# Query and key parts kept in one DRAM region each: a stack is fetched by one transfer of two runs of rows instead of by two transfers

## The chip, the cores and the metric

The kernel runs on one core of a Trainium2 chip. The metric is the device time of one execution in microseconds; the time of a kernel is the median of its runs. The engines of the core have names in the profile: PE does matrix products (PEld is its loading of weights, which runs beside the products), DVE and ACT do vector work, POOL and SP mostly issue transfers. A transfer (DMA) is issued by one engine into a queue of that engine and is carried by up to 16 DMA engines that all queues share.

## The reference, cut to what matters

Two layers of an encoder over 512 tokens of width 1024, in float32. Each layer is a SwiGLU feed-forward block of width 2816 at half weight, a mixer, and a second such block, each between two RMS norms. The mixer is what the change touches:

```
proj = u @ w_in            # q, k, v of three attention branches, and three gates
A: neighbourhood attention, 8 heads of 64, with a relative position bias
B: sliding window attention, 8 query heads and 2 key/value heads of 64, window 128
C: differential attention, 4 heads, two softmax maps each, rotary positions
m   = sum_i gate_i * (branch_i @ W_branch_i)
h   = h + post(m @ W_out)
```

## The kernel before, in words

**Precision.** Each float32 operand of a product is split into a high part `hi`, rounded to a narrower type that PE multiplies fast, and a low part `lo`, the rest. A product is then hi·hi + hi·lo + lo·hi: three matmuls (L326 to L328), mostly of 128 rows against 512 columns. The feed-forward blocks and most projections go through a scheme with fewer block products (L680), the gates of the mixer through the plain one (`dense1`, L345).

**Stacks.** A head has 64 rows (its width) and 512 columns (the tokens). Since 64 is half of PE's 128 rows, scores are made with *stacks*: tiles `st` of 128 rows with the 64 rows of `hi` of one head above the 64 rows of `lo` of the same head. A key head has a second stack with the two the other way round. One query stack against the two key stacks then gives all the products that are wanted, in two matmuls (L1675).

**From projection to mixer.** `project` makes the query, key and value parts of a layer, each 128 rows (two heads) by 512 tokens. For the first query and key part of branch A (`QA`, `KA`) it makes the stacks at once and leaves them on the chip, in slots called `early`. Every other part of branches A and B (queries QA+1 to QA+3 and QB to QB+3, keys KA+1 to KA+3 and KB) goes to DRAM by `stacked` (L1411): `store("part", hi)` and `store("part", lo)` put two regions of 128 rows, 256 KB each, by transfers that POOL issues (L1405). `mixer` fetches them: `restacked` (L1774) makes each stack with two transfers of 64 rows (128 KB), both issued by SP (L1783 the upper half, L1784 the lower half). A layer fetches 14 query stacks and 16 key stacks, so it issues 60 such transfers. Values are read whole (`values` and `load`, L1757), the relative position tables of branch A by `ask` (L1729, tile `braw`): each as 128 rows of 2 KB which the source gives as 8 runs of 16 rows. The query and key parts of branch C are stored whole, and `rope` (L1763) reads them as one transfer `x <- raw` and four `sh <- raw`, and turns them on DVE (L1769).

**What sets the order.** The mixer's units stand in a string `ORDER` (L93): `qa1` fetches what the second pair of heads of branch A needs, `aa1` computes them, `ga0` is a block of gates, `kb` and `qb0` fetch the key and the first query part of branch B, and so on. A scheduler orders the instructions of each engine by a model of their durations, so that dense gate products lie between the steps of an attention head. Once built, the order on an engine is fixed: an engine that has to wait at an instruction doesn't take up a later one. SP issues its transfers in order too, and there are eight semaphores in turn for the transfers that SP and ACT issue: a transfer waits until the one eight places earlier has landed. Weights (`wr`, 512 KB) are issued by ACT during the mixer (L211). There are 14 buffers `st`.

`softmax_pv` holds the steps of one attention head: scores (L1675), bias and row minimum on DVE (L1678), exponentials on ACT, transposes on PE (L1706), a split into `hi` and `lo` (L353 for `lo`), and the products with the values (L1709 with `hi`, L1710 with `lo`).

Of the kernel before, what the change touches and what calls it, by code (L numbers as in the profile page):

```python
# [10 lines left out]
F32 = mybir.dt.float32  # L11
# [5 lines left out]
P = 128  # L17
# [3 lines left out]
T = 512  # L21
# [18 lines left out]
QA, KA, VA, QB, KB, VB, QC, KC, VC, GL = 0, 4, 8, 12, 16, 17, 18, 22, 26, 30  # L40
# [79 lines left out]
def encoder_kernel(ctx: ExitStack, tc: tile.TileContext, order, xT, wts, cols, rows, rpb, consts, tables, out):  # L120
    nc = tc.nc
# [5 lines left out]
    dr = ctx.enter_context(tc.tile_pool(name="dr", bufs=1, space=bass.MemoryType.DRAM))  # L127
# [19 lines left out]
    def nm(s):  # L147
        serial[0] += 1
        return f"{s}{serial[0]}"

    def big(tag, dt=F32, shape=(P, T), name="v"):
        if tag in BUFS:
            return sb.tile(list(shape), dt, tag=tag, name=nm(name), bufs=BUFS[tag])
        kind, pool = phase[0]
        return pool.tile(list(shape), dt, tag=tag, name=nm(name), bufs=ABUFS[kind][tag])
# [7 lines left out]
    V, A, G, PE = nc.vector, nc.scalar, nc.gpsimd, nc.tensor  # L163

    def f(t):
        return t.bitcast(F32)
# [94 lines left out]
    for l in range(L):  # L261
        for which in (1, 2):
            name = f"ffn{which}_w_down"
# [1104 lines left out]
    def project(l, op, accs):  # L1368
# [34 lines left out]
        def store(kind, x):  # L1403
            d = dr.tile([P, T], F32, tag=kind, name=nm(kind), bufs=60)
            G.dma_start(d, f(x))  # L1405
            return d

        def parts(x):
            hi, lo = big("t", F32R, name="hi"), big("t", F32R, name="lo")
            A.activation(hi, x, AF.Copy)  # L1410
            V.tensor_tensor(out=lo, in0=x, in1=f(hi), op=ALU.subtract)  # L1411
            return hi, lo

        def stacked(c, x):
            hi, lo = parts(x)
            if c in (QA, KA):
                made[c] = []
                for s in range(2):
                    own, res = slice(64 * s, 64 * s + 64), []
                    for one, two in ((hi, lo), (lo, hi))[: 1 if c == QA else 2]:  # L1420
                        st = slots.pop(0)
                        nc.sync.dma_start(f(st)[0:64], f(one)[own])
                        nc.sync.dma_start(f(st)[64:128], f(two)[own])
                        res.append(st)
                    made[c].append((res + [None])[:2])
                return
            made[c] = store("part", hi), store("part", lo)

        def turned(c, x, heads):
            tp = bank("at")  # L1430
# [19 lines left out]
        def turned_by(c, x):  # L1450
            sh = big("t", name="sh")
            for q in range(4):
                o = q ^ 1
                nc.sync.dma_start(sh[32 * q : 32 * q + 32], x[32 * o : 32 * o + 32])
            slowly.extend(
                (
                    lambda: V.tensor_tensor(out=x, in0=x, in1=turning[0], op=ALU.mult),
                    lambda: V.tensor_tensor(out=sh, in0=sh, in1=turning[1], op=ALU.mult),
                    lambda: V.tensor_tensor(out=x, in0=x, in1=sh, op=ALU.add),
                    lambda: stacked(c, x),  # L1460
                )
            )

        def ready(c, x):
            if c >= GL:
                gated(c, x)
            elif c < VA:
                stacked(c, x)
            elif QB <= c < VB:
                turned_by(c, x)  # L1470
            elif c < KB or c >= VB and (c < QC or c >= VC):
                values.append(lambda: turned(c, x, 1 if c >= VC else 2))
            else:
                made[c] = store("raw", x)
# [11 lines left out]
        made = {}  # L1486
# [38 lines left out]
        for n, c0 in (("cosR", 0), ("sinR", 512)):  # L1525
            t = big("rr", name=n)
# [25 lines left out]
        def tables_of_a():  # L1552
            t = sb.tile([P, 4, T], F32, tag="n", name=nm("pre"), bufs=BUFS["n"])
            nc.sync.dma_start(t[:, 0, :], tables[:, 1024 : 1024 + 512])
            nc.sync.dma_start(t[:, 1, :256], tables[:, 1024 + 512 : 1024 + 768])
            for hd in range(2):
                nc.sync.dma_start(t[:, 2 + hd, :], raw_of(l, hd))
            made["tables"] = t
            made["edges"] = sb.tile([P, 4, T], F32, tag="n", name=nm("edges"), bufs=BUFS["n"])
# [75 lines left out]
        work(len(slowly))  # L1635
        return made

    def raw_of(l, hd):
        return bass.AP(rpb.tensor, (l * 8 + hd) * 16 * RPBW, [[RPBW, 8], [1, 16], [1, 8 * RPBW]])

# [76 lines left out]
    def mixer(l, op, made):  # L1717
# [6 lines left out]
        def ask(hd):  # L1724
            if hd < 2:
                raws[hd] = pre[:, 2 + hd, :]
                return
            raw = raws[hd] = big("g", name="braw")
            nc.sync.dma_start(raw, raw_of(l, hd))  # L1729
# [44 lines left out]
        def restacked(c, both):  # L1774
            if c in (QA, KA):
                return made[c]
            hi, lo = made[c]
            res = []
            for s in range(2):
                own, pair_ = slice(64 * s, 64 * s + 64), []  # L1780
                for one, two in ((hi, lo), (lo, hi))[: 2 if both else 1]:
                    st = big("st", F32R, name="st")
                    nc.sync.dma_start(f(st)[0:64], one[own])  # L1783
                    nc.sync.dma_start(f(st)[64:128], two[own])  # L1784
                    pair_.append(st)
                res.append((pair_ + [None])[:2])
            return res
# [20 lines left out]
        def qkv_a(p):  # L1808
            got = restacked(QA + p, False), restacked(KA + p, True), values(VA + p)
            for s in range(2):  # L1810
                ask(2 * p + s)
            return got
# [124 lines left out]
        def qkv_b(c):  # L1937
            return restacked(c, c == KB)
# [69 lines left out]
        at = len(order) // HB  # L2008
# [62 lines left out]
    for l in range(L):  # L2071
        with open_phase("f"):
            X, accs = ffn(l, 1, X, accs)
        with open_phase("p"):
            made = project(l, X, accs)
# [10 lines left out]
def build(order):  # L2086
    import concourse.bacc as bacc

    nc = bacc.Bacc("TRN2", target_bir_lowering=False, num_devices=1)
    shapes = {  # L2090
        "xT": (D, T),
        "wts": (NTILES, P, WB * P),
        "cols": (P, NCOLS),
        "rows": (L * ROWW,),
        "rpb": (L * 8 * 16 * RPBW,),
        "consts": (P, CONSTW),
        "tables": (P, TABLEW),
    }
    args = [nc.dram_tensor(f"in_{n}_dram", s, F32, kind="ExternalInput").ap() for n, s in shapes.items()]
    args.append(nc.dram_tensor("out_0_dram", (D, T), F32, kind="ExternalOutput").ap())  # L2100
    with tile.TileContext(nc) as tc:
        encoder_kernel(tc, order, *args)
    return nc
# [35 lines left out]
```

## Time and profile before

| what | value |
|---|---|
| time, median of 3 runs | 2371.69 us (2371.62 to 2374.82) |
| the profiled execution's own time | 2370.88 us |
| its span in the trace | 2369.1 us |
| instructions in the trace | 40269 |
| granted TensorE clock, mean | 0.996 |
| DMA over the span | 395.16 MB, mean 167 GB/s |
| stack transfers issued by SP, both layers | 120 of 128 KB |

The page gives busy times of the engines over the span, then the span cut into 40 slices, then the DMA queues, then the chain of work that ended last, then groups of instructions by line. The queue `q1` is SP's, `q10` ACT's, `q0` POOL's. In the table of stretches of time each engine has its busy time with the number of instructions, and behind them stand the granted clock of PE, the mean busy share of the 16 DMA engines, and GB/s. In the list of instructions in order of time a row has the start, the duration, the engine, the line, the operation, output and inputs, the shapes, and in square brackets how long the engine was idle before it and what ended that.

The two layers run the same program. The first score from a fetched stack of branch A starts at 531.18 us in the first layer and at 1703.59 us in the second, 1172.41 us later.

### The profile page before, as it was taken

What the parts mean: (1) busy time and instruction counts of PE and PEld (TensorE: products, weight loads), DVE (VectorE), ACT (ScalarE), POOL (GpSimd) and SP (SyncE); (2) the same over time, 40 slices, a digit from 0 to 9 for tenths busy, and PEclk for the clock granted to TensorE, in tenths of its full rate; (3) what the DMA queues carried; (4) which work ended last, traced back from release to release, by engine and by line L of the source; (5) the groups of instructions that cost most, each with busy time, mean ns of one, the idle gap of its engine ahead of it and who ended that gap; (6) DMA issues with size and microseconds to landing.
All of it is one profiled execution on the core that took longest, in us unless ns stands there. A gap on an engine that the chain in (4) does not pass through costs nothing. (4 is left out here: it accounts for less than half of the span.)

```text
span 2369.1 us, 40269 instructions
## 1 busy us (share of the span) xinstructions
PE 2342.6 (99%) x15134; PEld 2109.5 (89%) x15134; DVE 1892.4 (80%) x3082; ACT 1446.8 (61%) x2715; POOL 223.8 (9%) x354
## 2 busy tenths in 40 slices
PE   9999999999999999999999999999999999999998
PEld 8999889997888889998899998889978788899987
DVE  7887988966888668888878878889579876788796
ACT  6555566667777465655655554666687764556563
POOL 0111001110121001110001110011101200011100
PEclk9999999999999999999999999999999999999999
DMA  5566446667565524664525565276774664256642
GB/s 170 162 169 190 154 145 187 207 219 207 168 174 189 167 97 147 166 162 165 175 87 168 162 178 196 102 216 199 222 206 139 195 206 140 97 147 172 190 148 84
DMA packets 138147, 395.16 MB, mean 167 GB/s; under 512 B 19296, under 2 KB 26080, under 8 KB 137440
## 3 DMA queue, kind: packets, MB, share of 16 engines
q1 hardware_dynamic: 102960, 260.37, 35.0%
q0 software_dynamic: 20160, 78.66, 12.4%
q10 hardware_dynamic: 14832, 53.56, 7.4%
q8 instruction: 119, 1.95, 0.3%
q14 instruction: 76, 0.62, 0.1%
HBM read 326.98 MB, written 80.74 MB: 172 GB/s over the span
## 5 line engine op out<-in xcount | busy, mean ns | idle before, releaser
L680 PE MATMUL mm<-X,h 128*128 128x256 f32 x1504 | 268.0, 278 | 1.2 <-DVE v L738 1.2
L680 PEld LDWEIGHTS mm<-X,h 128*128 128x128 f32 x1504 | 228.5, 188 | 2.5 <-DVE v L738 2.0
L225 DVE TENSOR_TENSOR w<-wr,w 128x512 fp32r<-128x512 f32 x264 | 178.9, 685 | 56.2 <-ACT w L224 55.2
L224 ACT ACTIVATE w<-wr 128x512 fp32r<-128x512 f32 x264 | 162.5, 627 | 96.4 <-PE mm L328 40.8
L326 PE MATMUL mm<-X,w 128*128 128x512 f32 (+1 forms) x570 | 218.3, 383 | 1.8 <-ACT X L553 1.8
L328 PE MATMUL mm<-X,w 128*128 128x512 f32 (+1 forms) x570 | 216.4, 380 | 0.8 <-DVE w L225 0.8
L327 PE MATMUL mm<-X,w 128*128 128x512 f32 (+1 forms) x570 | 216.2, 379 | 0.8 <-DVE X L554 0.7
L680 PE MATMUL mm<-ht,h 128*128 128x256 f32 x752 | 210.1, 279 | 0.0
L680 PE MATMUL mm<-ht,l 128*128 128x256 f32 x752 | 210.1, 279 | 0.0
L680 PE MATMUL mm<-lt,h 128*128 128x256 f32 x752 | 209.4, 278 | 0.0
L680 PE MATMUL mx<-ht,h 128*128 128x256 f32 x752 | 208.3, 277 | 0.6 <-ACT v L724 0.6
L680 PE MATMUL mm<-X,l 128*128 128x256 f32 x752 | 208.2, 277 | 0.0
L680 PE MATMUL mx<-ht,l 128*128 128x256 f32 x752 | 208.1, 277 | 0.0
L680 PE MATMUL mx<-lt,h 128*128 128x256 f32 x752 | 207.9, 277 | 0.0
L630 DVE TENSOR_TENSOR l<-wr,h 128x1024 fp32r<-128x1024 f32 x94 | 114.9, 1222 | 65.7 <-PE mm L680 65.7
L662 ACT ACTIVATE h<-wr 128x1024 fp32r<-128x1024 f32 x94 | 99.9, 1062 | 78.7 <-PE mx L680 55.5
L680 PE MATMUL at<-X,w 128*128 128x256 f32 x1128 | 144.2, 277 | 0.0
L680 PEld LDWEIGHTS mx<-ht,h 128*128 128x128 f32 x752 | 141.2, 188 | 1.4 <-ACT v L724 1.4
L680 PEld LDWEIGHTS mm<-ht,l 128*128 128x128 f32 x752 | 141.7, 188 | 0.1
L680 PEld LDWEIGHTS mm<-ht,h 128*128 128x128 f32 x752 | 141.7, 188 | 0.0
L680 PEld LDWEIGHTS mm<-lt,h 128*128 128x128 f32 x752 | 141.7, 188 | 0.0
L680 PEld LDWEIGHTS mx<-ht,l 128*128 128x128 f32 x752 | 141.2, 188 | 0.2 <-DVE l L640 0.2
(458 smaller groups left out, 6802.4 us busy)
## 6 DMA issues: line engine op xcount, KB each, us to landing
wr<-in_wts_dram SPq DMA_DIRECT2D x273, 512.0 KB, 4.6
wr<-in_wts_dram ACTq DMA_DIRECT2D x102, 512.0 KB, 4.1
sum<-in_wts_dram POOLq DMA_DIRECT2D x64, 512.0 KB, 5.3
st<-part SPq DMA_DIRECT2D x120, 128.0 KB, 5.1
ap<-in_wts_dram SPq DMA_DIRECT2D x20, 512.0 KB, 5.6
a<-kept SPq DMA_DIRECT2D x32, 256.0 KB, 6.3
ap<-sum SPq DMA_DIRECT2D x16, 512.0 KB, 4.3
x<-part SPq DMA_DIRECT2D x32, 256.0 KB, 3.8
```

The lines of the kernel that those rows point to most:

```text
L224: A.activation(hi, raw, AF.Copy)
L225: V.tensor_tensor(out=lo, in0=raw, in1=f(hi), op=ALU.subtract)
L326: PE.matmul(acc, w[0], x[0], start=start, stop=False)
L327: PE.matmul(acc, w[0], x[1], start=False, stop=False)
L328: PE.matmul(acc, w[1], x[0], start=False, stop=stop)
L630: V.tensor_tensor(out=w["l1"], in0=self.raws[g][0], in1=f(w["h1"]), op=ALU.subtract)
L662: A.activation(self.W[g]["h24"], self.raws[g][1], AF.Copy)
L680: PE.matmul(acc, ws[i], xs[j], start=start and k == m == 0, stop=stop and k == n - 1 and m == 2, skip_group_check=True,)
```

## The change

The two regions `part` of a query or key part become one region `both`, with `hi` in rows 0 to 127 and `lo` in rows 128 to 255; a key part has a third piece, `hi` again, in rows 256 to 383. POOL puts each piece by a transfer of its own. A stack of head s is then read from the region by one transfer: rows 64s to 64s + 63 of one piece and the same rows of the next piece, which lies 128 rows behind. For the swapped stack of a key the reading starts one piece later (lo, then the second copy of hi). `halves` writes that source as an access pattern of three levels: 2 runs, 64 rows of each, 512 columns of each. The transfer's target is the whole tile `st` of 128 rows.

```diff
@@ stacked
-            made[c] = store("part", hi), store("part", lo)
+            n = 2 + (KA <= c < VA or c == KB)
+            d = dr.tile([n * P, T], F32, tag=f"both{n}", name=nm("both"), bufs=60)
+            for at, t in enumerate((hi, lo, hi)[:n]):
+                G.dma_start(d[P * at : P * at + P], f(t))
+            made[c] = d
@@ project, mixer
+    def halves(d, row):
+        pitch = d.ap[0][0]
+        return bass.AP(d.tensor, d.offset + row * pitch, [[P * pitch, 2], [pitch, 64], [1, T]])
@@ restacked
-            hi, lo = made[c]
             res = []
             for s in range(2):
-                own, pair_ = slice(64 * s, 64 * s + 64), []
-                for one, two in ((hi, lo), (lo, hi))[: 2 if both else 1]:
+                pair_ = []
+                for n in range(2 if both else 1):
                     st = big("st", F32R, name="st")
-                    nc.sync.dma_start(f(st)[0:64], one[own])
-                    nc.sync.dma_start(f(st)[64:128], two[own])
+                    nc.sync.dma_start(f(st), halves(made[c], P * n + 64 * s))
                     pair_.append(st)
                 res.append((pair_ + [None])[:2])
             return res
```

A layer's 60 stack transfers of 128 KB become 30 of 256 KB, with the same bytes read, and POOL issues 4 stores more (the second copies of KA+1 to KA+3 and KB). Lines behind L1427 carry higher numbers in the changed kernel: L1675 becomes L1683, L1706 becomes L1714, L1709 and L1710 become L1717 and L1718, L1729 becomes L1737, and the stack transfer is L1790.

The scheduler places instructions anew. On SP, at the start of the first layer's mixer, these transfers follow each other before the change (`braw` are the position tables of branch A, `st` the stacks of its third pair of heads):

```order
L1729 DMA braw_5944<-in_rpb_dram 128x1x512
L1783 DMA st_6125<-part_4444 64x512
L1784 DMA st_6125<-part_4446 64x512
L1783 DMA st_6128<-part_4444 64x512
L1784 DMA st_6128<-part_4446 64x512
L1783 DMA st_6131<-part_4457 64x512
L1784 DMA st_6131<-part_4459 64x512
L1783 DMA st_6134<-part_4459 64x512
L1784 DMA st_6134<-part_4457 64x512
```

The same place on SP in the changed kernel, with the next `braw` as its last row:

```order
L1737 DMA braw_5931<-in_rpb_dram 128x1x512
L1790 DMA st_6112<-both_4443 128x1x512
L1790 DMA st_6114<-both_4443 128x1x512
L1790 DMA st_6116<-both_4455 128x1x512
L1790 DMA st_6118<-both_4455 128x1x512
L1790 DMA st_6120<-both_4455 128x1x512
L1790 DMA st_6122<-both_4455 128x1x512
L1737 DMA braw_6128<-in_rpb_dram 128x1x512
```

Each pair of rows has become one, and the six stacks stand directly between two position tables. On PE the order moves as well. Before, the products with the values of an early head (`hi` or `lo` against `early`) are followed by dense gate products (`mm`):

```order
L1709 MATMUL o_6186<-hi_6190,early_3957 128x2x128
L1710 MATMUL o_6186<-lo_6191,early_3957 128x2x128
L1709 MATMUL o_6186<-hi_6199,early_3957 128x256
L1710 MATMUL o_6186<-lo_6200,early_3957 128x256
L328 MATMUL mm_6302<-X_3648,w_6106 128x512
L326 MATMUL mm_6302<-X_3648,w_6106 128x512
L327 MATMUL mm_6302<-X_3649,w_6106 128x512
L328 MATMUL mm_6302<-X_3648,w_6106 128x512
L1709 MATMUL o_6186<-hi_6208,early_3957 128x256
```

In the changed kernel, at the same place:

```order
L1717 MATMUL o_6167<-hi_6171,early_3957 128x2x128
L1718 MATMUL o_6167<-lo_6172,early_3957 128x2x128
L1717 MATMUL o_6167<-hi_6180,early_3957 128x256
L326 MATMUL mm_6283<-X_3648,w_6093 128x512
L327 MATMUL mm_6283<-X_3649,w_6093 128x512
L1683 MATMUL mx_6149<-st_5917,st_5913 128x256
L1683 MATMUL mx_6149<-st_5919,st_5913 128x256
L328 MATMUL mm_6283<-X_3648,w_6093 128x512
L1683 MATMUL mx_6153<-st_5917,st_5913 128x256
L1683 MATMUL mx_6153<-st_5919,st_5913 128x256
```

The scores of the next heads (`mx`, from fetched stacks) have moved ahead of dense products. The same holds up to the first scores of branch B: from the first score out of a fetched stack to the first score of `qb0`, PE has 133 dense matmuls of 512 columns, 91 matmuls of 256 and 44 of 128 before the change, and 84, 92 and 46 after it. Both layers are moved in the same way.

## Prediction, before the changed kernel was run

> **What bounds the kernel now.** I read the page first, then the waits of PE and the list of PE's instructions around the longest of them, then SP's transfers and the stretches of time about the start of the mixer.
>
> ```profile
> span 2369.1 us, 40269 instructions
> PE 2342.6 (99%) x15134; PEld 2109.5 (89%) x15134; DVE 1892.4 (80%) x3082; ACT 1446.8 (61%) x2715; POOL 223.8 (9%) x354
> q1 hardware_dynamic: 102960, 260.37, 35.0%
> ```
>
> PE is busy for 2342.6 of 2369.1 us: only 26.5 us of idling can be won, and every wait that is added to PE is paid in full, since its order is fixed and it has no slack elsewhere. SP's queue q1 uses the 16 DMA engines to 35.0% on the mean, so on the mean there is room. PE's waits that have to do with the mixer's loads:
>
> ```profile
> PE o L1710 <- DVE lo L353: 6.9, 2, 3.7
> ```
>
> That is two waits, one in each layer, 6.9 us together. The list of PE's instructions about them, the first layer's and then the second's, and what DVE and SP did then:
>
> ```profile
> 540.63 0.40 PE L328 MATMUL mm<-X,w 128*128 128x512 f32 x1
> 540.86 0.39 PE L326 MATMUL mm<-X,w 128*128 128x512 f32 x1
> ...
> 557.87 0.58 PE L1710 MATMUL o<-lo,x 128*128 128x256 f32 x1 [3.67 <-DVE lo L353]
> ...
> 559.11 0.63 PE L327 MATMUL mm<-X,w 128*128 128x512 f32 x1
> ...
> 563.36 0.40 PE L328 MATMUL mm<-X,w 128*128 128x512 f32 x1
> 1729.85 0.39 PE L1710 MATMUL o<-lo,x 128*128 128x256 f32 x1 [3.21 <-DVE lo L353]
> 548.06 0.43 SPq L1760 DMA_DIRECT2D x<-raw  x1
> 556.73 0.69 DVE L1769 TENSOR_TENSOR x<-x,cosR 128x512 f32<-128x512 f32 x1 [5.60 <-DMA x<-raw]
> 550.00:560.00 10.00, 6.33 (x30) 5.09 (x31) 3.00 (x11) 5.76 (x19) 0.00 (x0) 0.83 1.00 247
> ```
>
> `x<-raw`, issued at 548.06, came so late that DVE stood at its rotation for 5.60 us, until 556.73, with the split `lo` that PE needed queued behind it. PE stood for 3.67 us and then ran at a lower granted clock (0.83 in that stretch). A dense product starts 0.23 us after the one before (540.63 to 540.86) when PE runs freely; from 559.11 to 563.36 ten of them took 4.25 us, 1.95 more than 2.3. So the stall costs 3.67 + 1.95 = 5.6 us in the first layer and 3.21 + about 1.95 = 5.2 in the second: 10.8 us, and it comes from late loads.
>
> **The change part by part.** *Fewer issues.* SP issues 30 transfers less in each layer. What an issue takes on SP, the two-run one by the nearest row, a load in runs, and POOL's stores:
>
> ```profile
> L1783 SPq DMA_DIRECT2D st<-part x60: 444/504/1117, 495.2 to 1769.5; - x60
> L1729 SPq DMA_DIRECT2D braw<-in_rpb_dram x12: 622/643/665, 526.5 to 1733.4; - x12
> L1405 POOL DMA_DIRECT2D part<-hi x30: 542/542/599, 375.1 to 1686.8; - x30
> ```
>
> Instead of 60 × 0.504 = 30 us SP spends some 30 × 0.643 = 19 us in a layer. That shortens no row of PE by itself: SP's 11 us lie beside PE's work, and are worth at most what the stall is, 10.8 us for both layers. The 4 stores more in a layer are 4 × 0.54 = 2.2 us on POOL, busy for 9%; they are made during the projection, under PE's products. Nothing for them.
>
> *Who carries a two-run load.* The bytes loaded are the same; what decides is over how many DMA engines a transfer is spread. No two-run load is in the trace. The nearest are `braw` (128 rows of 2 KB in 8 runs of 16 rows) and the old stack halves (64 plain rows). Two `braw` are issued at 526.52, and stacks behind them from 528 on. Stretches of 2.5 us, a look at the emptiest microsecond, and the landing times of stacks issued from 524 to 528 and from 528 to 532:
>
> ```profile
> 526.52 1.39 SPq L1729 DMA_DIRECT2D braw<-in_rpb_dram  x2
> 526.00:528.50 2.50, 2.50 (x14) 2.06 (x13) 0.60 (x2) 2.50 (x10) 0.00 (x0) 1.00 0.90 275
> 528.50:531.00 2.50, 2.50 (x14) 2.12 (x14) 0.58 (x2) 2.50 (x8) 0.54 (x1) 1.00 0.90 71
> 530.00:531.00 1.00, 1.00 (x6) 0.80 (x5) 0.58 (x2) 1.00 (x5) 0.00 (x0) 1.00 0.28 51
> 531.00:533.50 2.50, 2.50 (x20) 2.32 (x20) 2.31 (x5) 2.27 (x7) 0.54 (x1) 1.00 0.95 316
> ...
> st<-part SPq DMA_DIRECT2D x3, 128.0 KB, 2.6
> st<-part SPq DMA_DIRECT2D x4, 128.0 KB, 8.1
> ```
>
> With `braw` in the queue the rate falls from 275 to 71 GB/s and comes back to 316. At 530 to 531 only 0.28 × 16 = 4.5 engines are busy, though loads stand in the queue, and stacks behind it take 8.1 us instead of 2.6. So a load given in 8 runs isn't spread over all engines; my reading is that each run goes to one engine as a piece, 8 runs to at most 8 engines. By the same reading two runs go to two engines, and these carry 131 kB each for every stack, one behind the other. I assume the same two each time: since the rate fell with two `braw` in the queue, loads in runs don't seem to take turns over all engines (if they did, many stacks in the queue would keep all sixteen busy). That bounds the cost from both sides: 16 engines, as for plain rows (no cost), and 2 engines (each 8 times as long busy). I take 2: `braw` is of the changed load's kind, a source of three levels, and the old halves are not.
>
> [...]
>
> *The price of a kB on one engine.* Three rows: a saturated stretch later in the layer, the page's q1, and the mixer's start.
>
> ```profile
> 1940.00:1950.00 10.00, 10.00 (x51) 7.78 (x49) 4.38 (x8) 5.34 (x10) 0.00 (x0) 1.00 1.04 390
> DMA packets 6938, 14.06 MB, mean 220 GB/s; under 512 B 1104, under 2 KB 1104, under 8 KB 6933
> q1 hardware_dynamic: 5750, 9.88, 59.3%
> st<-part SPq DMA_DIRECT2D x44, 128.0 KB, 4.5
> braw<-in_rpb_dram SPq DMA_DIRECT2D x6, 256.0 KB
> ```
>
> 390 GB/s over 16 engines are 24.4 GB/s, 41 ns per kB. The page's q1 gives 0.35 × 16 × 2369.1 us / 260,370 kB = 51 ns; q1 in the stretch 516 to 580 us gives 0.593 × 16 × 64 / 9,880 = 61 ns, with loads in each other's way. With 14 engines nearly idle there is less in the way: I take 45, and 41 and 61 as ends.
>
> *What the two engines have to carry.* The last four rows above are of the stretch 516 to 580 us, which holds what the mixer needs up to the first scores of `qb0`: 44 halves, which are 22 stacks. On each of the two engines: 22 × 131.1 = 2884 kB of stacks; of all else (14.06 − 5.77 = 8.29 MB) a sixteenth, 518 kB; and since the six `braw` lie on 8 engines, another 98 kB. Together 3500 kB. At 45 ns that is 157.5 us (143.5 at 41; 213.5 at 61).
>
> ```profile
> 516.27 0.44 SPq L1783 DMA_DIRECT2D st<-part  x1
> 531.18 0.28 PE L1675 MATMUL mx<-st,st 128*128 128x256 f32 x1
> 531.30 0.28 PE L1709 MATMUL o<-hi,early 128*128 128x256 f32 x1
> ...
> 580.11 0.48 PE L1675 MATMUL mx<-st,st 128*128 128x256 f32 x2
> L1675 PE MATMUL mx<-st,st x74: 276/332/442, 577.9 to 646.8; 128*128 128x256 f32 x42, 128*128 128x384 f32 x32
> ```
>
> The stacks start at 516.27, so the last one that `qb0` needs lands at about 673.8. When would PE want it? The first score from a fetched stack is at 531.18. From there to `qb0`, the changed order has 84 matmuls of 512 columns (0.23 us each), 92 of 256 (0.12, by 531.18 to 531.30) and 46 of 128 (half of that, an estimate): 19.3 + 11.0 + 2.8 = 33.1 us, so 564.3. The same sum for the order before (133, 91 and 44) gives 44.2, with the stall's 5.6 581.0, and the trace has `qb0`'s scores at 580.11: the method holds. PE is late by 673.8 − 564.3 = 109.5 us in a layer. Dense products can't fill that, as PE doesn't take up a later row, and those that the new order has put behind the scores come after the wait.
>
> *Behind `qb0`* eight stacks are left at most, each 131.1 kB × 45 ns = 5.9 us, while the scores of branch B's eight heads are spread over 577.9 to 646.8, 8.6 us a head. With the sixteenth of all else on the two engines it about balances; I add nothing and keep up to 12 us a layer for the upper end.
>
> *The sum.* 2 × 109.5 = 219 us of waiting, less the 10.8 us of the old stall, which the new wait contains: 2370.9 + 208 = 2579, in the profiled execution's own time of 2370.88 us. The median of the three runs is 0.8 us above that: **2580 us**. With 41 ns the wait is 95.5 us a layer: 2552. With 51 it is 130.5: 2622; with 61, 2693.
>
> **The rivals.**
> *All 16 engines carry the two-run load (faster).* The target is a tile of 128 plain rows, like that of `x`, and if the target decides, a stack lands as the halves did. For it: a stack is one transfer of 256 KB, and fewer queue behind each other. Against it: `braw` has the same target, and it held up the queue. Then late `x<-raw` goes, which the new order puts later on DVE too, and with it the 10.8 us: 2361, chance 0.05. [...]
>
> *No change.* All engines carry it, but the stall goes over to another load of the crowded start, a position table or the first key of `qb0`, wanted some 16 us earlier: 2371, chance 0.04.
>
> *Eight engines, as for `braw` (slower, by little).* If the pieces are smaller than a run, 22 × 32.8 + 616 = 1337 kB lie on the busiest engine, 60 us at 45 ns. The last stack is there at 576.5, 12 us behind 564.3; less 5.4 us, twice: about 2384, chance 0.07. It decides once an engine's share passes 48 us / 45 ns = 1070 kB.
>
> **How the numbers follow.** The forecast has 0.84. Its range: 41 ns gives 2552, and some of the rest can be moved behind `qb0`, which takes off 20; at the other end 51 ns gives 2622, and branch B adds 2 × 12 and stacks that hinder each other more, up to the 61 ns end at 2693, which I don't take in full: 2530 to 2680. A change of 0.2% (4.7 us) is about what a measurement of this kernel can tell from none. Faster by more: 0.05; within: 0.04; slower: 0.84 + 0.07 = 0.91.
>
> **What would show it.** In the profile after, PE waits at L1683 for `st`, some 100 us a layer, its busy share falls to about 91%, and the slices at the start of both mixers show GB/s of 50 to 100. A stack takes several times 5 us from issue to landing, and issues of SP wait for the transfer eight places earlier. The wait at L1718 for `lo` is gone or small. It is wrong if stacks land within 3 to 6 us at 200 GB/s or more: then all engines carry them; or if the waits lie at DVE's rotation or bias with `st` in time. If the wait is there but of another size, the price per kB or the ledger is the term at fault.

## The result, and the profile after

The changed kernel takes 2579.29 us (median of 5 runs, 2578.99 to 2584.57), the kernel before beside it 2371.62: a ratio of 1.0888, 95% interval 1.0868 to 1.0908. It is slower by some 208 us, about 104 in each layer. The profiled execution took 2579.29 us, with a span of 2577.5.

The page of the changed kernel, its first lines and the row of SP's queue:

```profile
span 2577.5 us, 40225 instructions
PE 2381.7 (92%) x15134; PEld 2138.8 (83%) x15134; DVE 1899.2 (74%) x3082; ACT 1448.5 (56%) x2715; POOL 226.0 (9%) x362
PEclk9999999977899999999999999999678999999999
q1 hardware_dynamic: 101160, 260.36, 31.5%
```

PE's idle time went from 26.5 to 195.8 us, which is 169.3 of the 208.4 us that the span grew. The other 39.1 stand in PE's busy time (2342.6 to 2381.7 with the same 15134 matmuls): the row PEclk shows it at 6 to 8 tenths of its clock in two places, the starts of the two mixers. A matmul that starts alone also counts as busy for longer than one in a row (0.40 us, where the next one starts after 0.23 us in the kernel before), so how much of the 39.1 us is the clock isn't separated. Bytes on SP's queue are the same as before. The waits of PE, and DVE's longest for a load:

```profile
PE mx L1683 <- DMA st<-both: 89.2, 15, 20.9
PE mx L1683 <- DVE nmx L1686: 45.8, 6, 12.8
PE o L1717 <- ACT hi L352: 18.0, 2, 9.0
PE o L1717 <- DVE o L1721: 15.4, 2, 8.5
PE o L1718 <- DVE lo L353: 6.0, 4, 3.1
```

```profile
DVE bedge L1752 <- DMA braw<-in_rpb_dram: 70.3, 6, 21.1
```

The first row is PE waiting for stacks. The rest I read as the same lateness on a longer way: DVE waits 70.3 us for position tables that are queued behind stacks, and PE waits for what DVE and ACT make after that. Who carries the stacks is read from a stretch in which nothing else runs, and from the issues on SP:

```profile
574.00:576.00 2.00, 0.00 (x0) 0.00 (x0) 0.00 (x0) 0.00 (x0) 0.00 (x0) 0.98 0.13 50
647.00:661.00 14.00, 0.00 (x0) 0.00 (x0) 0.00 (x0) 0.00 (x0) 0.00 (x0) 0.50 0.21 73
```

```profile
L1790 SPq DMA_DIRECT2D st<-both x60: 490/5100/8902, 494.7 to 1963.8; - x60
```

From 574 to 576 us no engine works, stacks and position tables are queued, and the 16 DMA engines are busy to 0.13 on the mean: 0.13 × 16 = 2 engines, at 50 GB/s, 25 GB/s each. From 647 to 661 PE does nothing at all for 14 us. An issue of a stack takes 5.1 us on SP in the median (0.504 before): as I read it, SP is held up until the two engines have taken work off the queue.

### The profile page after: what moved, and what is told of

Read it like the earlier page. It is cut to its first block, busy times and chain, and to the rows that moved or that the text cites. A ratio compares the mean times of both kernels' runs of the same rounds, so it can differ in the third digit from the quotient of the medians.

```text
span 2577.5 us, 40225 instructions
## 1 busy us (share of the span) xinstructions
PE 2381.7 (92%) x15134; PEld 2138.8 (83%) x15134; DVE 1899.2 (74%) x3082; ACT 1448.5 (56%) x2715; POOL 226.0 (9%) x362
## 3 DMA queue, kind: packets, MB, share of 16 engines
q1 hardware_dynamic: 101160, 260.36, 31.5%
## 5 line engine op out<-in xcount | busy, mean ns | idle before, releaser
L680 PE MATMUL mm<-X,h 128*128 128x256 f32 x1504 | 268.1, 278 | 2.5 <-DVE v L738 2.5
L680 PEld LDWEIGHTS mm<-X,h 128*128 128x128 f32 x1504 | 228.4, 188 | 3.8 <-DVE v L738 3.1
L326 PE MATMUL mm<-X,w 128*128 128x512 f32 (+1 forms) x570 | 222.2, 390 | 2.4 <-ACT X L553 1.8
L327 PE MATMUL mm<-X,w 128*128 128x512 f32 (+1 forms) x570 | 221.3, 388 | 0.8 <-DVE X L554 0.7
L328 PE MATMUL mm<-X,w 128*128 128x512 f32 (+1 forms) x570 | 218.3, 383 | 0.0
L680 PE MATMUL mm<-ht,h 128*128 128x256 f32 x752 | 210.6, 280 | 2.3 <-ACT at L719 2.2
L680 PE MATMUL mm<-ht,l 128*128 128x256 f32 x752 | 210.1, 279 | 0.0
L680 PE MATMUL mm<-lt,h 128*128 128x256 f32 x752 | 209.4, 278 | 0.0
L680 PE MATMUL mx<-ht,h 128*128 128x256 f32 x752 | 208.3, 277 | 0.3 <-ACT v L724 0.2
L680 PE MATMUL mm<-X,l 128*128 128x256 f32 x752 | 208.2, 277 | 0.0
L680 PE MATMUL mx<-ht,l 128*128 128x256 f32 x752 | 207.9, 276 | 0.0
L680 PE MATMUL mx<-lt,h 128*128 128x256 f32 x752 | 207.9, 276 | 0.0
L1683 PE MATMUL mx<-st,st 128*128 128x256 f32 (+1 forms) x224 | 62.0, 373 | 135.1 <-DMA st<-both 89.2
L1683 PEld LDWEIGHTS mx<-st,st 128*128 128x128 f32 x224 | 46.6, 236 | 145.9 <-DMA st<-both 60.1
L680 PEld LDWEIGHTS mm<-ht,h 128*128 128x128 f32 x752 | 141.6, 188 | 3.0 <-ACT at L719 3.0
L680 PE MATMUL at<-X,w 128*128 128x256 f32 x1128 | 144.1, 277 | 0.0
L352 ACT ACTIVATE hi<-at 128x256 fp32r<-128x256 f32 (+2 forms) x160 | 69.9, 443 | 130.1 <-PE at L1714 61.2
L680 PEld LDWEIGHTS mx<-ht,h 128*128 128x128 f32 x752 | 141.3, 188 | 0.8 <-ACT v L724 0.7
```

The lines of the kernel that those rows point to most:

```text
L326: PE.matmul(acc, w[0], x[0], start=start, stop=False)
L327: PE.matmul(acc, w[0], x[1], start=False, stop=False)
L328: PE.matmul(acc, w[1], x[0], start=False, stop=stop)
L352: A.activation(hi, src, AF.Copy)
L680: PE.matmul(acc, ws[i], xs[j], start=start and k == m == 0, stop=stop and k == n - 1 and m == 2, skip_group_check=True,)
L1683: PE.matmul(shaped(sp, k), qs, k, start=m == 0, stop=m == 1)
```

## The experiments

Two things changed at once: how a stack is read, and the order of instructions. The theory of the prediction (*engines*) is that a load whose source is two runs is carried by two DMA engines. Its rivals are *order* (the scores moved ahead of dense products ask for stacks too early), *region* (more stores, hi and lo in one region) and *merging* (one transfer of 256 KB is slow for its size).

### Changed stores, plain loads

```diff
-                    nc.sync.dma_start(f(st), halves(made[c], P * n + 64 * s))
+                    for m in range(2):
+                        at = P * (n + m) + 64 * s
+                        nc.sync.dma_start(f(st)[64 * m : 64 * m + 64], made[c][at : at + 64])
```

> The changed kernel's stores and regions, but each stack is again fetched by two transfers of 64 plain rows; the order on PE, DVE and ACT is then that of before. Theory of engines (a load in two runs is carried by two DMA engines): 2371 us, within 4 of the kernel before. Theory of order (the scores moved ahead of dense products ask for stacks too early): 2371 as well. Theory of the region (one region, four more stores in a layer, a conflict in memory): about 2580.

2364.93 us where the kernel before, run beside it, took 2368.07: ratio to before 0.9987 (0.9978 to 0.9995). The order on PE, DVE and ACT is that of before, and so is the profile:

```profile
span 2363.2 us, 40285 instructions
PE 2339.3 (99%) x15134; PEld 2106.3 (89%) x15134; DVE 1892.5 (80%) x3082; ACT 1447.0 (61%) x2715; POOL 227.1 (10%) x362
```

```profile
PE o L1718 <- DVE lo L353: 5.4, 2, 3.3
```

The region and its eight more stores cost nothing; the old stall is there again. Region is out. This is also the fastest kernel of the study, by 0.13%, too little to build on.

### Same change, rows outermost

```diff
-        return bass.AP(d.tensor, d.offset + row * pitch, [[P * pitch, 2], [pitch, 64], [1, T]])
+        return bass.AP(d.tensor, d.offset + row * pitch, [[pitch, 64], [P * pitch, 2], [1, T]])
```

> The changed kernel with one line edited: the source of a stack is written as 64 rows, two of each, instead of two runs of 64 rows, so that rows of hi and lo alternate in the stack, for queries and keys alike. Same bytes, same number of transfers, same order on every engine. Theory of engines: the slowest level is 64, all 16 engines carry it, the waits for stacks go and with them the old stall: about 2361 us (2355 to 2372). Theory of order, of the region, or of the one larger transfer: 2580 as the changed kernel.

2374.01 us, ratio 1.0026 (1.0014 to 1.0039). Bytes, transfers, sizes and the order on every engine are those of the changed kernel; only the two outer levels of the source are swapped, and 205 us are gone. That leaves neither order nor merging as the cause of the loss. The issue on SP is short again, and a stack lands in 6.3 us:

```profile
L1790 SPq DMA_DIRECT2D st<-both x60: 512/556/1292, 494.6 to 1758.6; - x60
```

```profile
st<-both SPq DMA_DIRECT2D x60, 256.0 KB, 6.3
```

But it is a miss as well: 2361 was expected, with the old stall of PE gone. The span and PE's waits in this kernel:

```profile
span 2371.1 us, 40225 instructions
PE o L1717 <- ACT hi L352: 4.8, 2, 2.4
PE o L1718 <- DVE lo L353: 2.9, 3, 2.1
```

The stall for `x <- raw` is gone, and in its place PE waits twice 2.4 us for `hi` and 2.9 us for `lo`. In the list of PE's instructions the first of these:

```profile
569.22 0.83 PE L1683 MATMUL mx<-st,st 128*128 128x256 f32 x4
572.46 0.38 PE L1717 MATMUL o<-hi,x 128*128 128x256 f32 x1 [2.41 <-ACT hi L352]
```

No dense product stands between these scores and the products with the values that follow, so PE reaches the latter before ACT has made `hi`. So the new order seems to cost about what it wins: it asks for heads early with less dense work between their steps. I have no run that separates the two.

### Four and eight runs, merged

The region is laid out in groups of rows (here 8 of hi, 8 of lo, 8 of hi); a stack is then k runs, in one transfer. For eight runs:

```diff
-                G.dma_start(d[P * at : P * at + P], f(t))
+                pitch, own = d.ap[0][0], 8 * at
+                G.dma_start(
+                    bass.AP(d.tensor, d.offset + own * pitch, [[24 * pitch, 16], [pitch, 8], [1, T]]), f(t)
+                )
...
-        return bass.AP(d.tensor, d.offset + row * pitch, [[P * pitch, 2], [pitch, 64], [1, T]])
+        return bass.AP(d.tensor, d.offset + row * pitch, [[24 * pitch, 8], [pitch, 16], [1, T]])
...
-                    nc.sync.dma_start(f(st), halves(made[c], P * n + 64 * s))
+                    nc.sync.dma_start(f(st), halves(made[c], 8 * n + 192 * s))
```

> The region is laid out in groups of 8 rows of hi, 8 of lo and 8 of hi, and a stack is one transfer of 8 runs of 16 rows; the order on every engine is that of the changed kernel. Theory of engines: 22 x 32.8 + 616 = 1337 kB on the busiest engine until the first scores of branch B, at 41.7 ns per kB (which the changed kernel showed) 55.8 us, 8 us late where the old stall cost 5.4: about 2376 us (2362 to 2388). Theory of order or of the one larger transfer: 2580.

2395.67 us, ratio 1.0115 (1.0096 to 1.0133): 20 us above the forecast. With groups of 16 rows:

> As the kernel with groups of 8 rows, with groups of 16: a stack is one transfer of 4 runs of 32 rows. Theory of engines: 22 x 65.5 + 616 = 2058 kB on the busiest engine, at 41.7 ns 85.8 us, 37.8 us late less 5.4, twice: about 2436 us (2420 to 2455). Theory of order or of the one larger transfer: 2580.

2467.0 us, ratio 1.0422 (1.0404 to 1.044): 31 above. The order of size is right, and neither is near 2580, but both miss their ranges. Against the kernel with rows outermost, which has the same order and which I had put 13 us too low, the misses shrink to some 7 and 18.

### Before's order, halves in two runs

Groups of 32 rows, and two transfers of 64 rows for each stack, each of two runs of 32:

```diff
-                    nc.sync.dma_start(f(st), halves(made[c], P * n + 64 * s))
+                    for m in range(2):
+                        nc.sync.dma_start(f(st)[64 * m : 64 * m + 64], halves(made[c], 32 * (n + m) + 192 * s))
```

> Two transfers of 64 rows per stack as before the change, in the order of before on PE, DVE and ACT, but the region is laid out in groups of 32 rows (hi, lo, hi), so that each transfer is two runs of 32 rows. Theory of engines: the same 131 kB a stack on two engines without any merging: the last stack that branch B's first scores need lands at 516 + 3500 x 0.0417 = 662 us, wanted at 575.4, 87 late, 12 more in branch B as in the changed kernel, less the old stall's 5.4, twice: about 2555 us (2530 to 2580). Theory that one merged transfer of 256 KB is slow, or that the changed order is: 2365.

2628.29 us, ratio 1.11 (1.108 to 1.112). Nothing is merged here and the order is that of before, and the loss is larger still, by 73 us more than the ledger gave. The waits show a second place, in the projection (`at` and the blocks of L680), and the stores take twice as long as in the kernel with plain loads (4.8 and 4.3 us there). The waits of PE, the stores (the last column is the time from issue to landing), and the first layer's projection up to the first load of a stack in bulk; in the last two, the rows behind the dots are those of the kernel with plain loads:

```profile
PE at L1439 <- ACT x L1398: 18.3, 2, 11.1
PE at L1439 <- DVE v L1446: 13.8, 2, 7.1
PE mm L680 <- DVE v L738: 8.5, 4, 4.7
```

```profile
both<-hi POOLq DMA_DIRECT2D x30, 256.0 KB, 9.4
both<-lo POOLq DMA_DIRECT2D x22, 256.0 KB, 11.1
...
both<-hi POOLq DMA_DIRECT2D x30, 256.0 KB, 4.8
both<-lo POOLq DMA_DIRECT2D x22, 256.0 KB, 4.3
```

```profile
330.00:516.00 186.00, 159.98 (x1139) 149.14 (x1138) 134.33 (x193) 100.48 (x190) 24.52 (x38) 0.95 0.54 155
...
330.00:516.00 186.00, 185.19 (x1407) 175.85 (x1406) 153.70 (x220) 120.51 (x226) 26.97 (x50) 1.00 0.59 190
```

The layout had put the *stores* into runs too (here four runs of 32 rows each). The first layer's projection fell behind: PE was busy for 159.98 of 186 us, against 185.19 in the kernel with plain loads. As I read it, the buffers of hi and lo came free late. So this kernel changes two things, which I hadn't meant, and so, in a smaller degree, does the one with groups of 16 rows (its stores land in 6.4 and 6.9 us); with groups of 8 the stores are 16 runs and land in 5.0 and 4.8 us, much as plain ones do. Loads and stores were therefore put into runs apart.

### Loads alone in runs of every k-th row

Regions and stores as in the changed kernel, two transfers per stack and the order of before; a half's source is k runs, each of every k-th row (the same for queries and keys). For k = 2:

```diff
-                        nc.sync.dma_start(f(st)[64 * m : 64 * m + 64], made[c][at : at + 64])
+                        nc.sync.dma_start(f(st)[64 * m : 64 * m + 64], halves(made[c], at))
...
-        return bass.AP(d.tensor, d.offset + row * pitch, [[P * pitch, 2], [pitch, 64], [1, T]])
+        return bass.AP(d.tensor, d.offset + row * pitch, [[pitch, 2], [2 * pitch, 32], [1, T]])
```

> The kernel of the first run (regions as changed, whole stores, two transfers of 64 rows per stack, order of before) with each half's source written as two runs of 32 rows, the even rows and the odd ones. Stores as in the changed kernel, so that only the loads are in runs. Theory of engines: 3500 kB on the busiest two at 41.7 ns, 146 us, last stack at 662, wanted at 575.4; 87 late, 12 in branch B, less 5.4, twice: about 2555 us (2530 to 2580). If the kernel with groups of 32 rows lost its further 73 us on the load side: about 2628.

> The same with four runs of 16 rows, every fourth row each. Theory of engines: 2058 kB x 41.7 = 85.8 us, last stack at 602.1, 26.7 late, less 5.4, twice: about 2410 us (2390 to 2425). Theory that any source in runs is slow alike: as with two runs.

> The same with eight runs of 8 rows. Theory of engines: 1337 kB x 41.7 = 55.8 us, last stack at 572.1, wanted at 575.4: not late, 2365 us (2362 to 2375). Theory that any source in runs is slow alike: as with two runs.

| runs in a source | us | ratio to before, 95% interval |
|---|---|---|
| plain rows (first kernel) | 2364.93 | 0.9987 (0.9978 to 0.9995) |
| 8 | 2374.03 | 1.0028 (1.0016 to 1.004) |
| 4 | 2427.61 | 1.0252 (1.0234 to 1.027) |
| 2 | 2569.97 | 1.0852 (1.0836 to 1.0869) |

Two of three lie in their ranges, four runs 3 us above its own. The order of PE is the same in all four rows. A quiet stretch with little but stacks in the queue, for 2, 4 and 8 runs in turn (DMA share and GB/s are the last two columns):

```profile
558.00:566.00 8.00, 5.57 (x25) 4.29 (x23) 1.81 (x3) 0.90 (x3) 0.00 (x0) 1.00 0.13 50
```

```profile
544.00:548.00 4.00, 4.00 (x19) 3.32 (x18) 2.05 (x3) 1.75 (x3) 0.00 (x0) 1.00 0.26 100
```

```profile
542.00:544.00 2.00, 2.00 (x10) 1.64 (x9) 0.76 (x2) 1.75 (x4) 0.00 (x0) 1.00 0.51 201
```

0.13, 0.26 and 0.51 of 16 are 2, 4 and 8 engines, at 50, 100 and 201 GB/s, 25 GB/s each. That is the prediction's reading, one engine for each run, measured here for 2, 4 and 8 runs.

### Stores alone in runs

```diff
-                G.dma_start(d[P * at : P * at + P], f(t))
+                for s in range(2):
+                    G.dma_start(odds(d, P * at + 64 * s), f(t)[64 * s : 64 * s + 64])
...
+        def odds(d, row):
+            pitch = d.ap[0][0]
+            return bass.AP(d.tensor, d.offset + row * pitch, [[pitch, 2], [2 * pitch, 32], [1, T]])
```

> The kernel of the first run with plain loads, but each piece is stored by two transfers of 64 rows, whose target is two runs of 32 rows (even rows, odd rows). Theory that slow stores in runs held up the projection in the kernel with groups of 32 rows: waits of PE at L1436 and for the blocks of the projection, 2385 to 2430 us. Theory that stores cost nothing in any form: 2365.

2426.58 us, ratio 1.025 (1.0231 to 1.027), with loads that are plain and an order that is that of before. The waits are again the projection's:

```profile
PE at L1441 <- ACT x L1398: 22.9, 2, 13.9
PE mm L680 <- DVE v L738: 11.4, 4, 7.9
```

```profile
both<-hi POOLq DMA_DIRECT2D x60, 128.0 KB, 9.1
both<-lo POOLq DMA_DIRECT2D x44, 128.0 KB, 9.9
```

So stores in runs cost some 60 us with loads that are plain. This kernel also makes twice as many stores, but the kernel with groups of 32 rows doesn't, and it lies 58 us above the one with two runs in the loads alone (2628.29 − 2569.97). The two sizes agree, and make up most of the 73 us by which the kernel with groups of 32 rows came out above the ledger.

### POOL issues the two-run loads

```diff
-                    nc.sync.dma_start(f(st), halves(made[c], P * n + 64 * s))
+                    G.dma_start(f(st), halves(made[c], P * n + 64 * s))
```

> The changed kernel with its stack transfers, two runs of 64 rows each, issued by POOL instead of SP; the order shifts in places. Theory that SP's queue gives every two-run load to the same two engines, while POOL's queue takes turns: most of the loss goes, 2365 to 2430 us. Theory that a two-run load is slow by itself, or that POOL uses one fixed pair too: 2540 to 2620.

2414.1 us (two runs), ratio 1.0196 (1.0171 to 1.0222). The same two-run loads, issued by POOL, lose 45 us where they lost 208. The row of POOL's queue in the stretch from 530 to 535 us (packets, MB, share of 16 engines), in which that queue has nothing but stacks in flight, and the time to landing over the whole run:

```profile
q0 software_dynamic: 272, 0.84, 75.9%
```

```profile
st<-both POOLq DMA_DIRECT2D x60, 256.0 KB, 13.2
```

One load still takes long (13.2 us), but now stacks alone keep 0.759 × 16 = 12 engines busy and move 0.84 MB in 5 us, 168 GB/s, where SP's queue gave them 2 engines and 50 GB/s. So it isn't the two-run load as such that costs 208 us: on SP's queue such loads all fall to the same two engines, one behind the other, and on POOL's they lie beside each other. What the other 45 us are made of isn't taken apart; the order of instructions also moved. Most of PE's waits are these:

```profile
PE o L1718 <- DVE lo L353: 19.6, 2, 10.7
PE mx L1683 <- DMA st<-both: 18.4, 7, 4.3
```

### The old stall alone

In the first kernel, the load of `x` in `rope` behind those of `sh`:

```diff
-            x = load(made[c])
             sh = big("tx", name="sh")
             for q in range(4):
                 o = q ^ 1
                 nc.sync.dma_start(sh[32 * q : 32 * q + 32], made[c][32 * o : 32 * o + 32])
+            x = load(made[c])
```

> The kernel of the first run (changed stores, two plain transfers per stack), with the load of x from raw in rope put behind the four loads of sh, so that DVE's rotation isn't placed ahead of its data. Theory that the old stall is DVE standing at its rotation for a late load, 10.8 us by the prediction's sum: about 2355 us (2352 to 2360) and no wait of PE for lo. Theory that the stall only moves to the next late load: 2363 to 2368.

2370.0 us, ratio 1.0008 (0.9997 to 1.0019): no gain, and a little above the second theory's range. PE's wait for `lo` at the old place is gone, yet the sum of the waits isn't lower:

```profile
span 2366.8 us, 40263 instructions
PE 2339.1 (99%) x15134; PEld 2104.6 (89%) x15134; DVE 1893.9 (80%) x3082; ACT 1445.4 (61%) x2715; POOL 226.2 (10%) x362
```

```profile
PE o L1900 <- DVE lo L353: 3.0, 2, 2.3
PE at L363 <- DVE nm L1876: 1.9, 2, 1.0
```

PE idles for 27.7 us against 23.9 in the kernel that it was made from; smaller waits have taken its place, among them these in branch C (L1900, `nm` of L1876). The scheduler places everything anew when a load moves, so this doesn't price the stall by itself.

## Why the prediction was right, point by point

The forecast was 2580, the result 2579.29. The mechanism is shown; that the total fits to 1 us is luck, since four terms were off and cancel.

**Who carries a two-run load.** Right: two engines, by the share in the trace and by the series 2, 4, 8 runs. But the rows of `braw` from which it was read don't show it. From 528.5 to 531 the engines were busy to 0.90 at 71 GB/s, so 16 × 0.90 engines shared 71 GB/s, 203 ns per kB, five times the 41 of the saturated stretch: they were slow rather than idle, and the one emptiest microsecond hid that. Why they were slow no run shows. That step was an estimate of mine, and as far as it rests on these rows it was luck. That they are the same two each time was an assumption; it holds on SP's queue. From 574 to 576 us, with three stacks in flight (issued at 557.19, 562.36 and 569.46), the rate stays at 50 GB/s, and they land one behind the other, at 578.49, 583.94 and 590.25. Of the position table issued behind them at 574.92, six of the eight pieces land by 583.43 and the last two after the third stack, at 590.58 and 591.58. The run with POOL shows the other case: 12 engines busy with stacks.

**The first scores of `qb0`.** Forecast: the last stack lands at 673.8 us. PE's row in the changed kernel, the stacks issued from 516 to 646 us (the one issued next is the last one needed), and all that was moved from 516 to 662 us:

```profile
661.97 1.41 PE L1683 MATMUL mx<-st,st 128*128 128x256 f32 x4 [20.85 <-DMA st<-both]
...
st<-both SPq DMA_DIRECT2D x21, 256.0 KB
...
DMA packets 6372, 13.63 MB, mean 93 GB/s; under 512 B 476, under 2 KB 476, under 8 KB 6366
```

It came at 661.97, 12 us earlier. The count of 22 stacks was right; all else was 13.63 − 22 × 0.262 = 7.9 MB instead of 8.29, so 491 + 98 kB, and with the stacks' 2884 that makes 3473 kB, close to the forecast's 3500. In 145.8 us (516.2 to 661.97) they cost 42.0 ns per kB, not 45: the price was the part that was too large, and the lower end, 41, was nearer.

The other end of the wait, 564.3, was too early. The kernel with rows outermost has the same order, and there these scores start at 569.22 (its row is shown above). The prediction's check of its sum took a wrong row: 580.11 is a score of an earlier head. Each of the six fetched heads of branch A has 8 scores; the 49th, `qb0`'s first, stands in the kernel before at

```profile
585.71 0.36 PE L1675 MATMUL mx<-st,st 128*128 128x256 f32 x1
```

where the sum gave 581.0. So PE was late by 661.97 − 569.22 = 92.75 us, not 109.5. The 575.4 us of the expectations came from the same sum.

**Behind `qb0`.** Forecast: it balances, nothing. It didn't:

```profile
710.00:730.00 20.00, 13.31 (x60) 11.80 (x61) 11.64 (x36) 7.28 (x22) 0.00 (x0) 0.74 0.22 61
```

PE idles for 6.7 of 20 us there, at 0.74 of its clock. Against the kernel with rows outermost the changed kernel's span is longer by 206.4 us (2577.5 − 2371.1), 103.2 in a layer. `qb0`'s lateness is 92.75 of that, so some 10 us were lost behind it: the term that I kept for the upper end (up to 12 us) and left out of the sum.

**The sum.** In a layer the forecast has 109.5 us of waiting, nothing behind it, and 5.4 us back from the old stall: 104.1. The runs have 92.75, some 10.4, and 1.0 us lost instead of 5.4 won (rows outermost against before, 2371.1 − 2369.1 in two layers): 104.2. The landing, the start without a wait, the part behind `qb0` and the stall were all off.

**The old stall.** It was taken as 10.8 us that go, whichever way. In the kernel with rows outermost, it is gone and the time is 2374, not 2361; in the run that removed it nothing was won. As the price of the rival "all 16 engines carry it" it was wrong: that rival would have come out at 2374, slower than before by 0.26%, not faster. What failed in it is the step that removing a wait in the middle of a mixer gives back its length: in both runs other waits had taken its place. Both also moved the order of instructions, so what the stall alone is worth stays open.

**The fewer issues.** SP's issues and POOL's stores cost and brought nothing, as said; but the 30 × 0.643 us put on SP for the new issues was wrong, as they took 5.1 us each while the queue was full. That did not matter by itself, since the two engines set the pace at which stacks came.

**What would show it.** PE's waits at L1683 for stacks and its share (92%, forecast about 91%) came, and 50 GB/s where little else is moved; the page's slices at the starts of the mixers have more, 76 to 128 GB/s. Three signs came otherwise. The waits at L1683 for `st` are 89.2 us in both layers together, not some 100 in each; the rest of the lateness stands in waits for DVE and ACT and in PE's busy time. The wait at L1718 for `lo` is not gone (6.0 us in four waits, 6.9 in two before). That a fifth of the loss would stand in PE's busy time was not in the text.

## What to carry to other kernels

Before two transfers are merged into one with a source of several levels, look at the outermost level of source and target: on SP's queue here, a level of 2 meant 2 of 16 DMA engines, the same two each time, and 50 GB/s. Here the same bytes could be had with the rows outermost, by letting rows of hi and lo alternate in the stack, which costs one line. Stores deserve the same look, and a mean load of a queue (35% before, 31.5% after) tells nothing of it: look at a stretch in which little but that load is in flight, at its share and its GB/s together, and at the bytes that the busiest engine has to carry until the first use.

## What the runs showed of the hardware that was not expected

- An issue on SP took 5.1 us in the median (8.9 at most) while stacks queued for two engines, against 0.556 with the same transfers, rows outermost, which landed in 6.3 us: as I read it, a long issue is a sign of a full queue, though the profile shows no wait there.
- The granted clock fell to between 0.50 and 0.98 in stretches in which PE stood still or idled for a third of the time or more (647 to 661 and 574 to 576 us; 0.74 from 710 to 730). PE's busy time is 39 us longer with the same matmuls; how much of that is the clock isn't separated.
- A store in two or four runs is slow on POOL's queue too (9.1 to 11.1 us instead of 4.3 to 4.8), and here that cost some 60 us in the projections of the two layers.
- POOL's queue carries many more small packets where its transfers are in few runs: the pages count 45344 under 512 B with the two-run loads and 43552 with the stores in two runs, where the changed kernel has 17624. Counted in the packed traces, they are 448 of 8 bytes for a load and 224 for a store: 14 times the 32 or 16 packets of 4 KB that each of two engines has of the data. Whether they are what makes these transfers slow isn't shown.
